# Openings of a two-layer encoder: who makes the first rests, which buffer holds the block that is fetched twice, when sums are requested, and the order of the second block product

## The chip, the cores and the metric

The kernel runs on one core of a Trainium2 chip. The metric is the time of one execution on the device, in microseconds (us). Three runs of the kernel before took 2184.75, 2187.49 and 2182.68 us, so the median is 2184.75 us. A further execution was recorded by the hardware profiler; all rows of traces below come from it.

## The reference, cut to what matters

A batch of one sequence with 512 frames of 1024 features gets 16 meta tokens in front (528 tokens) and goes through two layers, all in float32. Each layer is

```python
h = h + 0.5 * swiglu(rmsnorm(h, ffn1_norm[l]), ffn1_w_gate[l], ffn1_w_up[l], ffn1_w_down[l])
h = h + hybrid_mixer(rmsnorm(h, mix_norm[l]), w_in[l], ...)
h = h + 0.5 * swiglu(rmsnorm(h, ffn2_norm[l]), ffn2_w_gate[l], ffn2_w_up[l], ffn2_w_down[l])
```

where `swiglu(x, g, u, d)` is `(silu(x @ g) * (x @ u)) @ d` with an inner width of 2816, and the mixer multiplies its normed input by one wide matrix (queries, keys, values, two halves of a gated linear unit, two gates), runs stick-breaking attention and a gated convolution beside each other, and merges them. A last RMS norm follows, and the meta tokens are dropped.

## The kernel before, in words

**Precision.** The activations lie transposed, 8 tiles of 128 features by 528 tokens. Every float32 operand is split into a rounded part (`hi`) and the rest (`lo`), and a product is three matrix products: hi by hi, hi by lo, lo by hi. For activations the parts are called `uh`/`ul` (of the input), `sh`/`sl` (of sums of input pieces) and `ah`/`al` (of the inner layer); for weights `wh`/`wl`, in rings of four tiles each, 128 x 1024. A raw weight tile `wr` (a ring of three, 512 KB each) comes from HBM by a DMA that SyncE (SP) issues. ScalarE (ACT) rounds it (line 80, CAST wh<-wr). The rest comes in one of two ways. In `split` VectorE (DVE) subtracts (line 81, wl<-wr,wh). In the other way ACT writes the negated rounded part into `wl` (line 255) and GpSimd (POOL) issues a DMA that fetches the same weights from HBM a second time and adds them there (line 257, wl<-wg, wl<-wu or wl<-win). Mixer weights take the second way throughout.

**Seven products for eight.** The first two matrices of an FFN, and the value and gate halves of the mixer's linear unit, are computed in a scheme with seven block products. Input and weights are cut in two along the 1024 features and in column pairs, which gives weight blocks w11, w12, w21, w22 (each entry holds the block of both matrices, 8 x 128 columns). The seven weight operands are w11, s1 = w11 + w12, s2 = s1 + w22, w21, s3 = w12 + w22, w22, s4 = s2 + w21. A sum of two blocks is made by DMA: SP loads one block into a tile, POOL adds the other from HBM to it (line 207). The third block is added by DVE in place (line 267, s<-s,wr or wr<-wr). One block product is 24 matrix products of 264 columns (256 in the last FFN).

**The openings.** A new input is normed before each FFN or mixer, and what needs the norm factor can't be evicted at once. So at five places the first two column groups, numbered 0 and 1 here, are interleaved (`pair`, from line 422). Their w11 and w21 are called o11 and o21. The list `OPENING` (line 116) gives the order of the 14 block products; TensorE (PE) follows it as written:

o11 of 0, o11 of 1, o21 of 0, s1 of 0, s2 of 0, o21 of 1, w22 of 0, s3 of 0, s1 of 1, s4 of 0, s2 of 1, s3 of 1, w22 of 1, s4 of 1.

In the text they are o11_0, o11_1 and so on. The five openings are called A (mixer of layer 0), B (second FFN of layer 0), C (first FFN of layer 1), D (mixer of layer 1), E (second FFN of layer 1). The first FFN of layer 0 starts in another way.

After s2_n, DVE forms a combination from the PSUM accumulator in two halves (`opposite`, line 461: pe<-pb,q, or be<-bb,q in the mixer). The product w22_n accumulates on top of it, so PE can't start w22_n before both halves stand. The accumulator that `opposite` read is then written on by s3_n, so s3_n must wait for the two halves as well. `begin` (line 454) and `kept` (line 449) are ACT copies between accumulators.

**What sets the order.** Each engine runs its instructions in the order of its own list. PE's list is as written in the openings and in the mixer's attention. The other lists, and PE's in `down` (the FFN's second matrix), come from a scheduler that goes by priorities and its own estimates; `tc.add_manual_dep(..., NOSYNC)` puts one instruction behind another without a wait. Weights are prepared ahead by a walk over the list of products: `prep_unit` handles the product three places ahead (`LOOK`), and `fetch` keeps three raw tiles on their way or in use (`RAW`). In an opening the raw ring holds, in this order, o11_0, o11_1, o21_0, w11 for s1_0 (with w12 added by POOL), w22_0, o21_1, then w21 for s4_0 a second time, w22_1 and w21 for s4_1 a second time. s1_0 stays in its raw tile until s4_0. Sums s3_0, s1_1 and s3_1 go to tiles `s` of their own, requested by `fetch_sums` (line 230): s3_0 before the opening, s1_1 and s3_1 together, then the next quad's s1 and s3 together. In before.py the rests of o11_0, o11_1 and o21_0 are made by POOL's adding DMAs, that of o21_1 by DVE.

Of the kernel before, what the change touches and what calls it, by code (L numbers as in the profile page):

```python
# [13 lines left out]
P = 128  # L14
# [47 lines left out]
def kernel(ctx, tc, hT, par, const, wg1, wu1, wd1, win, wao, wco, wout, wg2, wu2, wd2, out):  # L62
# [35 lines left out]
    def fn(out, in_, func, **kw):  # L98
        need = SETS[func]
        if table["set"] != need:  # L100
            load = act.preload_act_table_set(need)
            for p in table["acts"]:
# [14 lines left out]
               ("s4", 0), ("s2", 1), ("s3", 1), ("w22", 1), ("s4", 1))  # L117
# [56 lines left out]
    state = {"prep": 0, "use": 0, "fetch": 0, "out": 0, "sums": 0}  # L174
# [14 lines left out]
    for n, (key, src, nk) in enumerate(units):  # L189
        at = key[1:]  # L190
        if nk == "w11":
            later_sums.append((n, ("s1", "s3")))
# [37 lines left out]
    def fetch_sums():  # L230

        n, names = later_sums[min(state["sums"], len(later_sums) - 1)]
        _, *at = units[n][0]
        if state["sums"] == len(later_sums) or tuple(at[:2]) != quads["of"]:
            return
        state["sums"] += 1
        for name in names:
            bufs = 1 if name == "s1" and at[0] == 2 else 2
            t = quads["pool"].tile([P, 8, P], F32, tag=name, bufs=bufs, name=name)
            load(t, n, "w11" if name == "s1" else "w22", "w12")  # L240
            raws[(name, *at)] = t

    def prep_unit():
# [7 lines left out]
        if nk not in QUAD:  # L251
            raw, nk0, nk = raws[key], nk, 8 if nk in OPEN else nk
            if key[0] in MIXER or nk0 == "o11" or nk0 == "o21" and units[n - 1][2] == "o11":
# [7 lines left out]
        else:  # L261
            at = key[1:]
            if nk == ("s1" if at in opened else "w11"):
                fetch_sums()
            if nk in ("s2", "s4"):
                x, y = raws[("s1", *at)], raws[("w22" if nk == "s2" else "w21", *at)]
                dve.tensor_tensor(out=x, in0=x, in1=y, op=ALU.add)  # L267
# [7 lines left out]
    def unit(*key):  # L275
        while state["prep"] < min(len(units), state["use"] + 1 + LOOK):
# [145 lines left out]
    def pair(ptile, sp, st, mode, of, ats, between, take, done):  # L422
# [23 lines left out]
        def kept(c):  # L446
            t = sp.tile([P, 2, TH], F32, tag="q", bufs=2, name="q")
            with priority(-URGENT):
                copies.append(act.copy(t, v(c)))
            return t  # L450

        def begin(c, t):
            with priority(-URGENT):
                copies.append(act.copy(v(c), t))

        copies = []
# [858 lines left out]
```

## Time and profile before

| | us |
|---|---|
| runs of the kernel before | 2184.75 (2182.68 to 2187.49) |
| the profiled execution, whole | 2186.04 |
| its span, first to last instruction | 2184.2 |
| PE busy | 2135.3 (98 %) |
| DVE busy | 1586.8 (73 %) |
| ACT busy | 1183.1 (54 %) |
| POOL busy | 534.4 (24 %) |

| opening | first to last product, us | length |
|---|---|---|
| A, mixer of layer 0 | 369.35 to 424.54 | 55.19 |
| B, second FFN of layer 0 | 740.38 to 788.09 | 47.71 |
| C, first FFN of layer 1 | 1100.92 to 1155.24 | 54.32 |
| D, mixer of layer 1 | 1467.54 to 1520.04 | 52.50 |
| E, second FFN of layer 1 | 1820.69 to 1871.15 | 50.46 |

The ends are the starts of the first product of the opening and of the first one behind it. In rows of waits the columns are total us, times, longest us. In rows of time the columns are start, duration, engine, line, operation, output<-input, shape; what stands in square brackets is the idle time of the engine just before it and what ended it. SPq is SP's queue of DMA issues.

### The profile page before, as it was taken

How to read it: one execution, taken by the hardware profiler on the slowest of the kernel's cores; microseconds unless marked ns; L12 is line 12 of the kernel's file. 1: busy time of each engine (PE TensorE's matmuls, PEld its weight loads, DVE VectorE, ACT ScalarE, POOL GpSimd, SP SyncE). 2: the span in 40 equal slices, each digit the busy share in tenths (PEclk: the TensorE clock that was granted, in tenths of full speed). 3: DMA queues.
4: the chain of work that ended last, by engine and by line, in shares of the span. 5: the costliest groups of instructions: out<-in, count | busy, mean ns of one | idle time of the engine just before them, and what ended most of it. 6: DMA issues, size and time to landing. Idle time of an engine off the chain costs nothing.

```text
span 2184.2 us, 40061 instructions
## 1 busy us (share of the span) xinstructions
PE 2135.3 (98%) x16058; PEld 2047.1 (94%) x16058; DVE 1586.8 (73%) x2221; ACT 1183.1 (54%) x1672; POOL 534.4 (24%) x499
## 2 busy tenths in 40 slices
PE   9999999999999999999989999999999999999998
PEld 9999999899999999999989999998888888899897
DVE  6867687777776677667877666877787767776685
ACT  6434356567776645343553443465678775343354
POOL 1322321311111231323123223213112112322220
PEclk9999999999999999999999999999999999999999
DMA  7465447765578957464395655367656789575532
GB/s 223 137 167 139 133 109 212 179 143 119 131 168 183 214 156 186 128 164 123 94 218 154 166 137 153 100 183 197 154 122 135 188 184 227 154 177 140 158 103 82
DMA packets 155290, 340.64 MB, mean 156 GB/s; under 512 B 17248, under 2 KB 21472, under 8 KB 155104
## 3 DMA queue, kind: packets, MB, share of 16 engines
q1 hardware_dynamic: 110928, 235.27, 34.2%
q0 software_dynamic: 43488, 102.26, 27.4%
q8 instruction: 126, 2.06, 0.4%
q10 hardware_dynamic: 688, 0.55, 0.1%
q14 instruction: 60, 0.49, 0.1%
HBM read 331.59 MB, written 6.42 MB: 155 GB/s over the span
## 4 chain that ended last, share of the span: by engine, by line
PE 89%; DMA 5%; DVE 3%; ACT 1%; issue 1%; SPq 0%; DVEq 0%; ACTq 0%; POOL 0%; POOLq 0%
PE pb L725 14%; PE ps L725 14%; PE ps L861 13%; PE ps L292 11%; PE ps L847 10%; PE pb L292 5%; PE pe L292 5%; PE pe L725 5%; DMA wr<-wu 2%; PE ps L443 1%; DMA wr<-win 1%; PE z L1043 1%; PE bs L443 1%; PE po L1087 1%; PE pe L443 1%
## 5 line engine op out<-in xcount | busy, mean ns | idle before, releaser
L80 ACT CAST wh<-wr 128x1024 fp32r<-128x1024 f32 (+4 forms) x284 | 251.6, 892 | 374.2 <-PE ps L292 90.7
L81 DVE TENSOR_TENSOR wl<-wr,wh 128x1024 fp32r<-128x1024 f32 (+4 forms) x284 | 312.6, 1103 | 62.4 <-ACT wh L80 59.1
L80 ACT CAST wh<-s 128x1024 fp32r<-128x1024 f32 x171 | 179.4, 1049 | 299.0 <-DVE s L267 85.8
L81 DVE TENSOR_TENSOR wl<-s,wh 128x1024 fp32r<-128x1024 f32 x171 | 233.0, 1362 | 52.5 <-ACT wh L80 50.1
L781 POOL TENSOR_TENSOR h<-h,dt 128x528 f32<-128x528 f32 (+1 forms) x96 | 177.7, 1858 | 268.4 <-DVE dt L779 268.4
L861 PE MATMUL ps<-uh,wh 128*128 128x264 f32 (+1 forms) x664 | 207.9, 313 | 0.3 <-DVE q L961 0.3
L861 PE MATMUL ps<-uh,wl 128*128 128x264 f32 (+1 forms) x664 | 203.6, 307 | 0.1
L861 PE MATMUL ps<-ul,wh 128*128 128x264 f32 (+1 forms) x664 | 203.7, 307 | 0.0
L207 POOL DMA_DIRECT2D s<-wg x81 | 73.1, 903 | 532.7 <-DMA s<-wg 202.0
L889 DVE SCALAR_TENSOR_TENSOR y<-uc,prm,y 128x528 f32<-128x528 f32 (+1 forms) x240 | 185.9, 811 | 0.5
L725 PE MATMUL ps<-ul,wh 128*128 128x264 f32 (+1 forms) x576 | 163.7, 284 | 0.0
L725 PE MATMUL pb<-sl,wh 128*128 128x264 f32 (+1 forms) x576 | 163.3, 283 | 0.0
L725 PE MATMUL ps<-uh,wl 128*128 128x264 f32 (+1 forms) x576 | 163.3, 283 | 0.0
L725 PE MATMUL pb<-sh,wl 128*128 128x264 f32 (+1 forms) x576 | 163.2, 283 | 0.0
L725 PE MATMUL pb<-sh,wh 128*128 128x264 f32 (+1 forms) x576 | 162.9, 283 | 0.0
L725 PE MATMUL ps<-uh,wh 128*128 128x264 f32 (+1 forms) x576 | 162.6, 282 | 0.0
L254 ACT CAST wh<-wr 128x1024 fp32r<-128x1024 f32 x103 | 108.0, 1049 | 95.1 <-PE ps L861 40.5
L292 PE MATMUL ps<-ah,wh 128*128 128x264 f32 (+1 forms) x616 | 142.7, 301 | 3.2 <-ACT wh L80 2.7
L292 PE MATMUL ps<-al,wh 128*128 128x264 f32 (+1 forms) x616 | 141.9, 300 | 0.5 <-DVE al L81 0.5
L292 PE MATMUL ps<-ah,wl 128*128 128x264 f32 (+1 forms) x616 | 141.7, 300 | 0.0
L861 PEld LDWEIGHTS ps<-uh,wl 128*128 128x128 f32 x664 | 125.0, 188 | 6.1 <-DMA wl<-win 0.3
L861 PEld LDWEIGHTS ps<-uh,wh 128*128 128x128 f32 x664 | 124.9, 188 | 6.2 <-issue 0.5
(402 smaller groups left out, 6918.1 us busy)
## 6 DMA issues: line engine op xcount, KB each, us to landing
wr<-wd SPq DMA_DIRECT2D x96, 384.0 KB, 3.6
wr<-wg SPq DMA_DIRECT2D x135, 256.0 KB, 3.5
wr<-wu SPq DMA_DIRECT2D x135, 256.0 KB, 3.8
wr<-win SPq DMA_DIRECT2D x56, 512.0 KB, 3.9
wl<-win POOLq DMA_DIRECT2D x56, 512.0 KB, 7.7
s<-wg SPq DMA_DIRECT2D x81, 256.0 KB, 4.8
s<-wu SPq DMA_DIRECT2D x81, 256.0 KB, 5.7
s<-wg POOLq DMA_DIRECT2D x81, 256.0 KB, 5.3
```

What stands on the lines that cost most here:

```text
L80: i = act.copy(hi, x)
L81: dve.tensor_tensor(out=lo, in0=x, in1=f(hi), op=ALU.subtract)
L207: queue.dma_start(raw[:, a:b], src, **kw)
L254: act.copy(hi[:, :nk], raw[:, :nk])
L292: pe.matmul(ps[:, c, :n], wt[:, k0 + k, :], xt[:, s:s + n], start=(k == 0 and pi == 0), stop=(k == end and pi == 2))
L443: pe.matmul(ps[:, e, :TH], wt[:, 4 * e + kk, :], xt, start=start and kk == 0 and pi == 0, stop=kk == KH - 1 and pi == 2, skip_group_check= ...
L725: pe.matmul(ps[:, e, :TH], wt[:, 4 * e + kk, :], xt, start=start and kk == 0 and pi == 0, stop=kk == 3 and pi == 2, skip_group_check=True)
L781: pool.tensor_tensor(out=tri(h[j], mode), in0=tri(h[j], mode), in1=tri(t, mode), op=ALU.add)
L847: pe.matmul(ps, wt[:, k0 + k, :], xt[:, s], start=(n == 0 and pi == 0), stop=(n == nk - 1 and pi == 2))
L861: pe.matmul(ps, wt[:, k, :], xt[:, s], start=(n == 0 and pi == 0), stop=(n == KD - 1 and pi == 2))
L889: t = dve.scalar_tensor_tensor(out=y, in0=uc[i][:, c0 + k:k + T], scalar=col(w0 + k), in1=y, op0=ALU.mult, op1=ALU.add)
L1043: pe.matmul(z[:, hh, :n], kk[r, ks], qq[r, q0:q0 + n], start=(pi == 0), stop=False, skip_group_check=True)
```

## The change

It has five parts, all on the openings, and one beside them.

1. The rests of o11_0 and o11_1 are made by `split`, so by DVE; ACT's negated copy and POOL's adding DMA for these two fall away. While these two units are asked for, the walk looks two places ahead and not three.
2. w21 for s4_0 is requested by `fetch_sums` into a tile `s` right behind s3_0, ahead of the opening, and no longer takes a raw tile. Tag s1 has two tiles everywhere, tag s3 one in the mixer. w21 for s4_1 is fetched at the place of s1_1 in the walk.
3. `fetch_sums` takes a count: s1_1 is requested when s2_0 is prepared, s3_1 with s3_0, and at s2_1 and s4_0 one and two sums of the quads that follow.
4. `OPENING` has s2_1 ahead of s4_0.
5. Three orders without waits: DVE's addition for s4 stands behind `opposite`; ACT's rounding of s2_0, s2_1 and s4_1 stands behind the last `begin`; that of s3_0 behind the norm's exponential (of s3_1 no longer).
6. `down` is issued on PE as written (but for each FFN's last group). On PE's list this moves four matrix products of `down` out of each of the openings B, C and E, where they stood ahead of s3_1, to the place behind the opening.

```diff
     OPENING = (("o11", 0), ("o11", 1), ("o21", 0), ("s1", 0), ("s2", 0), ("o21", 1), ("w22", 0), ("s3", 0), ("s1", 1),
-               ("s4", 0), ("s2", 1), ("s3", 1), ("w22", 1), ("s4", 1))
+               ("s2", 1), ("s4", 0), ("s3", 1), ("w22", 1), ("s4", 1))
+    WHEN = {("s2", "s1"): 1, ("s3", "w22"): 1, ("s4", "s2"): 2}
...
-        elif nk == "s1" and at in opened:
-            first = units[n - 1][2] in OPEN
-            later_sums.append((n, ("s3",) if first else ("s1", "s3")))
-            fetches += [(n, key, nk)] if first else []
-        elif at in opened and nk in ("s2", "s4"):
-            fetches.append((n, ("w22" if nk == "s2" else "w21", *at), "w22" if nk == "s2" else "w21"))
+        elif at in opened and nk in QUAD:
+            if nk == "s1" and units[n - 1][2] in OPEN:
+                later_sums += [(n, "s3"), (n, "w21")]
+                fetches.append((n, key, nk))
+            elif nk == "s1":
+                later_sums += [(n, "s1"), (n, "s3")]
+                fetches.append((n, ("w21", *at), "w21"))
+            elif nk == "s2":
+                fetches.append((n, ("w22", *at), "w22"))
...
+    def fetch_sums(count):
+
+        for n, name in later_sums[state["sums"]:state["sums"] + count]:
+            _, *at = units[n][0]
+            if tuple(at[:2]) != quads["of"]:
+                return
+            state["sums"] += 1
+            tag = "s3" if name == "s3" else "s1"
+            bufs = 1 if name == "s3" and at[0] == 2 else 2
+            t = quads["pool"].tile([P, 8, P], F32, tag=tag, bufs=bufs, name=tag)
+            load(t, n, *{"s1": ("w11", "w12"), "s3": ("w22", "w12")}.get(name, (name,)))
+            raws[(name, *at)] = t
...
-            if key[0] in MIXER or nk0 == "o11" or nk0 == "o21" and units[n - 1][2] == "o11":
+            if key[0] in MIXER or nk0 == "o21" and units[n - 1][2] == "o11":
                 act.copy(hi[:, :nk], raw[:, :nk])
                 act.activation(lo[:, :nk], raw[:, :nk], AF.Copy, scale=-1.0)
...
-            if nk == ("s1" if at in opened else "w11"):
-                fetch_sums()
+            if at in opened:
+                fetch_sums(WHEN.get((nk, units[n - 1][2]), 0))
+            elif nk == "w11":
+                fetch_sums(2)
             if nk in ("s2", "s4"):
                 x, y = raws[("s1", *at)], raws[("w22" if nk == "s2" else "w21", *at)]
-                dve.tensor_tensor(out=x, in0=x, in1=y, op=ALU.add)
+                i = dve.tensor_tensor(out=x, in0=x, in1=y, op=ALU.add)
+                if nk == "s4" and at in opened:
+                    tc.add_manual_dep(i.ins, state["opposite"].ins.name, NOSYNC, reason="behind the combination")
             i = split(raws[("s1" if nk in ("s2", "s4") else nk, *at)], hi, lo)
-            if nk == "s3" and at in opened:
-                tc.add_manual_dep(i.ins, state["rsqrt"].ins.name, NOSYNC, reason="behind the norm")
+            if at in opened and units[n - 1][2] in ("s1", "w22"):
+                behind = state["rsqrt" if nk == "s3" else "begin"]
+                tc.add_manual_dep(i.ins, behind.ins.name, NOSYNC, reason="behind the norm")
...
+        state["look"] = LOOK - 1
         ws = [unit("o11", *of, at) for at in ats]
+        state["look"] = LOOK
...
-                        down(gi)
+                        with tc.manual_schedule(engines={mybir.EngineType.PE}):
+                            down(gi)
```

**DVE in opening C, around the combination of group 0.** In the kernel before (s_13327 is s3_0, s_13338 is s1_1, the raw tile in `wr<-wr` is s1_0, to which w21 is added for s4_0):

```order
L81 TENSOR_TENSOR wl<-s_13327,wh 128x1024
L648 TENSOR_TENSOR up<-ps,g 128x264
L461 SCALAR_TENSOR_TENSOR pe<-pb,q 128x264
L267 TENSOR_TENSOR wr<-wr 128x1024
L461 SCALAR_TENSOR_TENSOR pe<-pb,q 128x264
L81 TENSOR_TENSOR wl<-s_13338,wh 128x1024
```

In the changed kernel (s_13333 is s3_0, s_13439 is s1_1, s_13338 now holds w21 for s4_0):

```order
L81 TENSOR_TENSOR wl<-s_13333,wh 128x1024
L469 SCALAR_TENSOR_TENSOR pe<-pb,q 128x264
L658 TENSOR_TENSOR up<-ps,g 128x264
L469 SCALAR_TENSOR_TENSOR pe<-pb,q 128x264
L81 TENSOR_TENSOR wl<-s_13439,wh 128x1024
L273 TENSOR_TENSOR wr<-wr,s_13338 128x1024
```

The addition for s4_0 moved from between the two halves of the combination to behind them. B and E read alike. In A and D, the mixer's openings, the rest of s1_1 stands between the two halves now:

```order
L81 TENSOR_TENSOR wl<-s_4579,wh 128x1024
L469 SCALAR_TENSOR_TENSOR be<-bb,q 128x264
L81 TENSOR_TENSOR wl<-s_4685,wh 128x1024
L469 SCALAR_TENSOR_TENSOR be<-bb,q 128x264
L273 TENSOR_TENSOR wr<-wr,s_4584 128x1024
```

Here s_4579 is s3_0, s_4685 is s1_1 and s_4584 is w21 for s4_0; the addition left that place in A and D too.

**POOL ahead of opening C.** In the kernel before (wl_13136 and wl_13209 are the rests of o11_0 and o11_1, wr_13141 is s1_0, wl_13263 the rest of o21_0, s3_13327 and s1_13338 the sums s3_0 and s1_1):

```order
L257 DMA wl_13136<-wg1 128x512
L257 DMA wl_13136<-wu1 128x512
L207 DMA wr_13141<-wg1 128x512
L207 DMA wr_13141<-wu1 128x512
L257 DMA wl_13209<-wg1 128x512
L257 DMA wl_13209<-wu1 128x512
L257 DMA wl_13263<-wg1 128x512
L257 DMA wl_13263<-wu1 128x512
L207 DMA s3_13327<-wg1 128x512
L207 DMA s3_13327<-wu1 128x512
L207 DMA s1_13338<-wg1 128x512
```

In the changed kernel (wr_13149 is s1_0, wl_13269 the rest of o21_0, s3_13333 and s1_13439 are s3_0 and s1_1):

```order
L211 DMA wr_13149<-wg1 128x512
L211 DMA wr_13149<-wu1 128x512
L261 DMA wl_13269<-wg1 128x512
L261 DMA wl_13269<-wu1 128x512
L211 DMA s3_13333<-wg1 128x512
L211 DMA s3_13333<-wu1 128x512
L211 DMA s1_13439<-wg1 128x512
```

Four adding DMAs of 256 KB each are gone from POOL's list ahead of each opening.

**SP in opening C.** In the kernel before (s3_13327 is s3_0, s1_13338 is s1_1, s3_13343 is s3_1, s1_13547 the next quad's s1, wr_13447 is w21 for s4_0, the fetch that stands first in the raw ring behind the sums):

```order
L207 DMA s3_13327<-wg1 128x512
L207 DMA s3_13327<-wu1 128x512
L207 DMA s1_13338<-wg1 128x512
L207 DMA s1_13338<-wu1 128x512
L207 DMA s3_13343<-wg1 128x512
L207 DMA s3_13343<-wu1 128x512
L207 DMA s1_13547<-wg1 128x512
L207 DMA s1_13547<-wu1 128x512
L207 DMA wr_13447<-wg1 128x512
L207 DMA wr_13447<-wu1 128x512
```

In the changed kernel (s1_13338 is w21 for s4_0, s1_13439 is s1_1, s3_13520 is s3_1, wr_13451 is w21 for s4_1):

```order
L211 DMA s3_13333<-wg1 128x512
L211 DMA s3_13333<-wu1 128x512
L211 DMA s1_13338<-wg1 128x512
L211 DMA s1_13338<-wu1 128x512
L211 DMA s1_13439<-wg1 128x512
L211 DMA s1_13439<-wu1 128x512
L211 DMA s3_13520<-wg1 128x512
L211 DMA s3_13520<-wu1 128x512
L211 DMA wr_13451<-wg1 128x512
L211 DMA wr_13451<-wu1 128x512
```

w21 for s4_0 moved up by three sums, s1_1 and s3_1 down by one place; the next quad's s1 stands behind these rows now.

More of the change, by code (lines that the diff above doesn't have):

```diff
@@ L173 @@
     RAW = 3
-    state = {"prep": 0, "use": 0, "fetch": 0, "out": 0, "sums": 0}
+    state = {"prep": 0, "use": 0, "fetch": 0, "out": 0, "sums": 0, "look": LOOK}
     ready, raws, counted = {}, {}, set()
@@ L275, in unit @@
     def unit(*key):
-        while state["prep"] < min(len(units), state["use"] + 1 + LOOK):
+        while state["prep"] < min(len(units), state["use"] + 1 + state["look"]):
             if units[state["prep"]][2] in QUAD and quads["pool"] is None:
@@ L460, in opposite @@
                 with priority(-URGENT):
[L461 to L462 removed]
+                    state["opposite"] = dve.scalar_tensor_tensor(out=out[:, e, :TH], in0=c[:, e, :TH], scalar=-1.0,
+                                                                 in1=q[:, e], op0=ALU.mult, op1=ALU.add)
         As = [ptile() for _ in range(2)]
+        state["look"] = LOOK - 1
         ws = [unit("o11", *of, at) for at in ats]
+        state["look"] = LOOK
         for ks in (range(KH - 1), (KH - 1,)):
@@ L470, in pair @@
         begin(Bs[0], v(As[0]))
-        between(ptile("pe"), copies[0])
+        between(ptile("pe"), state["begin"])
         Bs.append(kept(As[1]))
```

25 lines of the change are left out of this document (6 added, 19 removed).

## The prediction, made before any run of the changed kernel

> **What bounds the kernel now.** PE is busy for 98% of the span, so only its idle or slowed time can be won. I first read PE's waits over the whole span (total us, times, longest):
>
> ```profile
> PE pe L443 <- DVE pe L461: 12.2, 3, 4.9
> PE be L443 <- DVE be L461: 7.4, 2, 4.0
> PE bs L443 <- DMA wl<-win: 5.2, 4, 2.2
> PE ps L292 <- ACT wh L80: 2.7, 3, 0.9
> PE bs L443 <- DVE be L461: 2.0, 2, 1.0
> PE ps L443 <- DMA wl<-wg: 2.0, 1, 2.0
> ```
>
> Nearly all of it is line 443, the openings. Next I read one window per opening, A to E (start:end, length, busy time and instructions of PE, PEld, DVE, ACT, POOL, granted clock, DMA share, GB/s):
>
> ```profile
> 369.35:424.54 55.19, 47.50 (x343) 46.72 (x342) 39.35 (x63) 28.42 (x39) 15.30 (x19) 0.88 0.74 191
> 740.38:788.09 47.71, 43.10 (x344) 42.26 (x345) 36.53 (x56) 25.28 (x39) 12.18 (x14) 1.00 0.94 227
> 1100.92:1155.24 54.32, 47.16 (x346) 46.29 (x345) 38.15 (x59) 26.29 (x39) 12.36 (x14) 0.91 0.90 217
> 1467.54:1520.04 52.50, 45.29 (x343) 44.30 (x341) 38.97 (x59) 28.62 (x39) 15.38 (x18) 0.93 0.74 193
> 1820.69:1871.15 50.46, 44.30 (x341) 43.28 (x340) 37.00 (x57) 25.92 (x39) 12.25 (x14) 0.93 0.90 222
> ```
>
> The lengths add to 260.2 us, and B, which never lost the clock, is the shortest. The two largest rows of waits, 12.2 + 7.4 = 19.6 us, are one place in each opening, PE's first product of w22_0 (idle time ahead of it in brackets):
>
> ```profile
> 397.45 0.56 PE L443 MATMUL be<-sh,wh 128*128 128x264 f32 x1 [3.96 <-DVE be L461]
> 762.49 0.36 PE L443 MATMUL pe<-sh,wh 128*128 128x264 f32 x1 [3.30 <-DVE pe L461]
> 1127.44 0.56 PE L443 MATMUL pe<-sh,wh 128*128 128x264 f32 x1 [3.99 <-DVE pe L461]
> 1492.65 0.56 PE L443 MATMUL be<-sh,wh 128*128 128x264 f32 x1 [3.42 <-DVE be L461]
> 1843.89 0.55 PE L443 MATMUL pe<-sh,wh 128*128 128x256 f32 x1 [4.90 <-DVE pe L461]
> ```
>
> What DVE waited for there shows in C, from DVE's timeline:
>
> ```profile
> 1119.63 1.23 DVE L81 TENSOR_TENSOR wl<-s,wh 128x1024 fp32r<-128x1024 f32 x1 [0.58 <-ACT wh L80]
> ...
> 1121.12 0.43 DVE L461 SCALAR_TENSOR_TENSOR pe<-pb,q 128x264 f32<-128x264 f32 x1
> 1125.72 1.23 DVE L267 TENSOR_TENSOR wr<-wr 128x1024 f32<-128x1024 f32 x1 [4.17 <-DMA wr<-wu]
> 1126.86 0.43 DVE L461 SCALAR_TENSOR_TENSOR pe<-pb,q 128x264 f32<-128x264 f32 x1
> ```
>
> The first half of the combination stands at 1121.55, the second at 1127.29. Between them DVE's list holds the addition for s4_0, which no one needs yet; it waits 4.17 us for w21, fetched a second time. SP asked for that block late, once a raw tile was free:
>
> ```profile
> 1116.36 0.33 SPq L207 DMA_DIRECT2D wr<-wg  x1
> ```
>
> The wait costs more than its idle time. In the chain of waits the block product behind it takes 5.62 us where the next takes 3.02 us, a loss of 2.6 us; the first products of w22_0 in A, C, D and E are of the long kind (0.55 to 0.56 us), B's is not (0.36 us). The last row is s4_0:
>
> ```profile
> 1127.44 5.62 PE pe L443 x24
> 1133.06 3.02 PE pb L443 x24
> ...
> 1139.01 2.80 PE pb L443 x23
> ```
>
> **The change, part by part.** *1. w22_0 starts earlier* (own tile for w21 of s4_0, its addition behind both halves, fewer adding DMAs, o11 by DVE). Once that addition has left, what is late next is the rest of s3_0, which DVE makes ahead of the first half, and in A and D that of s1_1, now between the halves. Both follow an ACT rounding of a sum; these are the binding ones, s1_1 in A and D, s3_0 in B, C, E:
>
> ```profile
> 393.19 1.05 ACT L80 CAST wh<-s 128x1024 fp32r<-128x1024 f32 x1 [2.72 <-DMA s<-win]
> 755.23 1.05 ACT L80 CAST wh<-s 128x1024 fp32r<-128x1024 f32 x1 [1.92 <-DMA s<-wu]
> 1118.55 1.05 ACT L80 CAST wh<-s 128x1024 fp32r<-128x1024 f32 x1 [0.97 <-DMA s<-wu]
> 1490.19 1.04 ACT L80 CAST wh<-s 128x1024 fp32r<-128x1024 f32 x1 [2.85 <-DMA s<-win]
> 1838.96 1.04 ACT L80 CAST wh<-s 128x1024 fp32r<-128x1024 f32 x1 [5.62 <-PE ps L443]
> ```
>
> Four of them waited for the DMA that brings the sum. Lower bound, sums landing as before: in A the rounding ends at 394.24, the rest takes 1.23, the last half 0.43, so PE could start at 395.9 in place of 397.45, a gain of 1.5. D likewise: 1490.19 + 1.04 + 1.23 + 0.43 = 1492.9, so -0.2. In B, C and E three DVE pieces of 0.43 follow the rest (the row left out in C's fence is the third): C can start at 1118.55 + 1.05 + 1.23 + 1.29 = 1122.1, a gain of 5.3, E at 1842.5, a gain of 1.4. In B this gives 758.8, ahead of the end of o21_1 on PE (762.49 - 3.30 = 759.2), so the gain is its wait, taken as 3.5 with what moves ahead of it. Together 11.5.
>
> Upper bound: no wait is left, 19.6, and no slow product behind it, 4 x 2.6 = 10.4, so 30; with the stalls at o11, 5.2 + 2.0 = 7.2, it is 37.
>
> Between them decides what the DMA queues gain. In the 55 us of 1080 to 1135 they held (queue, packets, MB, share of the time of 16 engines):
>
> ```profile
> q0 software_dynamic: 2466, 4.49, 47.3%
> q1 hardware_dynamic: 3979, 7.24, 40.3%
> ```
>
> POOL's adding transfers (q0) cost 55 x 0.473 / 4.49 = 5.8 us per MB, SP's loads (q1) 55 x 0.403 / 7.24 = 3.1. The change drops two adding transfers of 0.52 MB ahead of each opening, 6.1 us, and puts w21 (0.52 MB, 1.6 us) ahead of s1_1: net 4.5 us. That counts where the queues are full, in A, C and D:
>
> ```profile
> 375.00:380.00 5.00, 4.49 (x22) 4.28 (x22) 3.59 (x7) 2.42 (x5) 0.00 (x0) 0.54 1.08 315
> 740.00:745.00 5.00, 4.62 (x38) 4.65 (x39) 4.82 (x7) 3.02 (x6) 0.00 (x0) 1.00 0.79 180
> 1093.00:1101.00 8.00, 8.00 (x68) 8.00 (x67) 6.25 (x12) 7.03 (x11) 5.28 (x6) 1.00 1.01 199
> ```
>
> At the starts of A and C the share is over 1.0, in B 0.79; the sums of B and E I leave where they land. I give A and D 3.0 us, two thirds of the relief, since part of it is spent ahead of transfers that are not late; so A gains 4.5 and D 2.8. In C the sums then come before o21_1 has ended (1127.44 - 3.99 = 1123.45); that end moves by the stall at o11_1 and its slow products:
>
> ```profile
> 1105.51 0.36 PE L443 MATMUL ps<-uh,wl 128*128 128x264 f32 x1 [2.00 <-DMA wl<-wg]
> 1106.05 0.42 PE L443 MATMUL ps<-uh,wl 128*128 128x264 f32 x1
> ```
>
> That is 2.0 of wait and about 0.8 of products, to 1120.6: C gains 6.8. Sum of the five: 4.5 + 3.5 + 6.8 + 2.8 + 1.4 = 19.0. The stalls at o11 lie ahead of w22_0 in the same opening, so they aren't counted again. To this comes the clock: 2.6 us in each of A, C and D, whose waits get short, 7.8 at most; I take 5, because a short wait can slow products too: behind the 2.00 us of C's o11 they took 0.42 us. E keeps 3.5 us of its wait and its slow product.
>
> The two added subtractions on DVE, 2 x 1.23 us, run ahead of each opening, where DVE is busy 6.25 of 8 us while PE is covered with other work, so I cost them at nothing; uncovered they cost up to 2.5 an opening (a rival below).
>
> The Trainium skill ("TensorE: Matmul & The Clock Gate", Part 1: The HAM clock gate) says that PE falls to half clock after an idle window of some 3.4 us. The rows agree in part: B's 3.30 us cost no clock, but 2.00 us did in C. By the page alone every wait that stays under 3.4 us would cost no clock, and the clock's gain would be 7.8 in place of 5, 10.4 if E's falls under it too, an estimate.
>
> *2. s2_1 ahead of s4_0.* s3_1 no longer follows directly on the halves of s2_1's combination; that hides the 2.0 us that A and D wait there. In B, C and E the 2.7 us of line 292 are matrix products of `down` that stood in the opening and waited for a weight; they leave it, for the place behind the opening, where I expect no such wait since the weight comes in its old order on ACT. Together 4.7. Against it: in A and D the query weights behind the opening take this chain, whose transfer's median landing stands in the page's list of issues (KB, us):
>
> ```profile
> 415.47 1.05 ACT L255 ACTIVATE wl<-wr 128x1024 fp32r<-128x1024 f32 x1
> 416.82 0.88 POOL L257 DMA_DIRECT2D wl<-win  x1 [2.42 <-ACT wl L255]
> ```
>
> ```profile
> wl<-win POOLq DMA_DIRECT2D x56, 512.0 KB, 7.7
> ```
>
> 416.82 + 7.7 (the median landing) = 424.5, just as A ends at 424.54: it is already due at its last moment, so the 1.0 us that s3_1 gains in each is waited for here instead. So 4.7 - 2.0 = 2.7.
>
> *3. `down` as written.* The products moved out run behind the opening instead: their PE time moves, 0.
>
> *4. s2_1 one place sooner.* Its weight is s1_1 plus w22_1, so it waits for w22_1's landing. In C DVE makes that sum here:
>
> ```profile
> 1129.20 1.22 DVE L267 TENSOR_TENSOR s<-s,wr 128x1024 f32<-128x1024 f32 x1 [0.43 <-DMA wr<-wu]
> ```
>
> s2_1 takes the place of s4_0, which PE began at 1139.0; with C's gain of 6.8 and its 2.6 of clock it is due at 1129.6. Sum, rounding and rest take 1.22 + 1.05 + 1.23 = 3.5. With the landing as now the weight stands at 1132.7, 3.1 late, the upper bound. But w22_1 now has the raw tile that w21 had, requested at 1116.36 and landed by 1125.72: ready at 1129.2, with 0.4 to spare, the lower bound 0. The second is nearer, since the raw ring does lose a fetch; I take -0.7.
>
> **Sum:** 19.0 + 5 + 2.7 - 0.7 = 26. The profiled execution took 2186.04 us (span 2184.2 and 1.8 around it), 1.3 over the median; so 2186.0 - 26 = 2160.0 there, and 2158.7, given as 2159, against the median.
>
> **Rivals.** *The wait changes hands.* The sums land no earlier than before, because SP and POOL hold other transfers ahead of them. Then w22_0 waits for s3_0 or s1_1, 11.5 is gained, the slow products stay, and with parts 2 and 4 (2.7 - 0.7) it is 13.5: 2184.75 - 13.5 = 2171. For it: four of the five roundings waited for their sum's DMA. Against it: the shares over 1.0.
>
> *All hidden.* The upper bound, 37, and 4.7 - 0.7, gives 41: 2144. For it: POOL loses four adding DMAs of 256 KB ahead of the sums. Against it: E's binding rounding ends at 1840.0, after which 1.23 + 1.29 must still run on DVE, so a wait of some 3.5 us there goes only if its sum lands sooner, for which no full queue speaks.
>
> *Slower: later sums.* In DVE's list the two added subtractions (2.5 us) stand ahead of the norm's sums (`nsum`, line 377), behind which SP asks for s3_0 and what follows. If they push that back in full, and w21 goes ahead of s1_1 (1.6), the sums come up to 4.1 us later in all five openings: 11.5 + 2.7 - 0.7 - 5 x 4.1 = -7, so 2192. It decides from 13.5 / 5 = 2.7 us on. Against it: DVE's 1.75 idle us of 8 ahead of C take most of the 2.5, and 6.1 us of dropped transfers outweigh 1.6.
>
> *It doesn't do what it says.* The transfer of w21 into its own tile waits for that tile's last reader and lands as late as before; then the addition moves but s4_0 waits for it, one place behind: the gain is 0 to 4.
>
> **Chances.** Forecast (2152 to 2168) 0.48; wait changes hands 0.20; all hidden 0.18; later sums 0.07; no effect 0.07. A measurement of this kernel tells about 0.2%, 4.4 us, from no change; so faster 0.48 + 0.20 + 0.18 = 0.86, the same 0.07, slower 0.07. The range takes in both neighbours, 2142 to 2174.
>
> **What would show it.** In the changed kernel the row of PE waiting for line 469 (461 before) should fall from 19.6 to below 7 us, DVE should make the two halves of the combination within 1 us of each other in B, C and E, and the opening windows should add to some 235 us with a clock near 1.00 in A, C and D. It is wrong if PE then waits as long for `wl` of s3_0 or s1_1 (first rival), if s3_1 or w22_1 show new waits above 1 us, if new waits come up behind the openings, or if `nsum` falls later against PE's o11_0 than before (the slower rival).

## The result, and the profile after

Four runs of the changed kernel took 2163.81 to 2170.57 us, median 2167.68, beside 2184.47 us for the kernel before: a ratio of 0.9921, with a 95% interval of 0.9901 to 0.994. The gain is 17 us where 26 were forecast, and the time lies at the upper edge of the forecast's 2152 to 2168. The profiled execution took 2168.47 us (span 2166.7), 17.6 less than that of before.

The five opening windows of the changed kernel, from the first product of each to the first one behind it (columns as in the prediction):

```profile
371.85:420.12 48.27, 43.99 (x343) 43.18 (x342) 39.77 (x64) 28.10 (x39) 14.18 (x19) 0.96 0.75 195
738.50:782.83 44.33, 42.00 (x341) 41.60 (x341) 36.34 (x56) 24.86 (x39) 10.52 (x12) 1.00 0.90 220
1098.05:1143.71 45.66, 43.17 (x343) 42.99 (x341) 37.83 (x59) 26.00 (x39) 11.37 (x13) 0.96 0.94 230
1458.32:1503.81 45.49, 42.59 (x343) 41.68 (x342) 39.52 (x59) 28.10 (x39) 12.25 (x18) 1.00 0.77 200
1806.38:1851.74 45.36, 40.78 (x339) 40.28 (x338) 36.39 (x57) 25.63 (x39) 11.36 (x13) 1.00 0.95 223
sum 229.11, PE 212.52 PEld 209.73 DVE 189.85 ACT 132.69 POOL 59.68; mean PE 42.50 PEld 41.95 DVE 37.97 ACT 26.54 POOL 11.94
```

They add up to 229.1 us where they were 260.2: 31.1 us gained. That is more than the 25 of the forecast's sign (some 235 us) and than the 28 that its terms inside the openings add to. The span is only 17.5 us shorter, so everything outside the openings is 13.6 us longer. PE's waits over the span of the changed kernel say what those are:

```profile
PE pe L452 <- DVE pe L469: 7.0, 3, 3.2
PE ps L301 <- DVE up L658: 5.0, 3, 1.9
PE ps L711 <- ACT wh L80: 4.9, 1, 4.9
PE ps L872 <- DMA wl<-win: 3.7, 2, 1.9
PE bs L452 <- ACT bs L463: 2.4, 2, 1.6
PE ps L452 <- ACT ps L463: 2.4, 2, 1.4
PE be L543 <- ACT nt L80: 1.9, 1, 1.9
PE ps L301 <- ACT ah L80: 1.6, 1, 1.6
PE be L452 <- DVE be L469: 1.4, 2, 1.2
PE be L543 <- DVE nt L81: 1.2, 2, 0.6
```

The first and the ninth row are w22_0's wait: 7.0 + 1.4 = 8.4 in place of 19.6. Two rows had no match before and lie behind the openings: `down` (line 301) waits 5.0 us for `up`, and the first query product (line 872) 3.7 us for the rest of its weights. Inside the openings s2_1 waits 2.4 + 2.4 for ACT's `begin` copy (line 463), and the norm's sum waits 3.1 for `nt` (line 543). The 4.9 us of line 711, the kernel's start, stood at 5.0 before.

The first product of w22_0 in the five openings of the changed kernel:

```profile
394.78 0.36 PE L452 MATMUL be<-sh,wh 128*128 128x264 f32 x1 [0.20 <-DVE be L469]
758.08 0.36 PE L452 MATMUL pe<-sh,wh 128*128 128x264 f32 x1 [1.34 <-DVE pe L469]
1118.68 0.36 PE L452 MATMUL pe<-sh,wh 128*128 128x264 f32 x1 [2.49 <-DVE pe L469]
1479.21 0.36 PE L452 MATMUL be<-sh,wh 128*128 128x264 f32 x1 [1.17 <-DVE be L469]
1827.27 0.36 PE L452 MATMUL pe<-sh,wh 128*128 128x256 f32 x1 [3.15 <-DVE pe L469]
```

Measured from the start of its opening, w22_0 begins earlier by:

| opening | before | after | gain | forecast |
|---|---|---|---|---|
| A | 28.10 | 22.93 | 5.2 | 4.5 |
| B | 22.11 | 19.58 | 2.5 | 3.5 |
| C | 26.52 | 20.63 | 5.9 | 6.8 |
| D | 25.11 | 20.89 | 4.2 | 2.8 |
| E | 23.20 | 20.89 | 2.3 | 1.4 |
| sum | | | 20.1 | 19.0 |

Outside the openings the kernel lost 2.5 us ahead of A, 2.5 behind A, 2.4 behind B, 2.3 behind C, 1.9 behind D and 1.9 behind E (lengths from the end of one opening to the start of the next). Of the losses behind B, C and E, 1.8 us in all are the products of `down` that left the openings (four of 264 columns in B and in C, two of 512 in E).

**Behind A** the changed kernel's rows of ACT, POOL and PE read:

```profile
410.83 1.05 ACT L80 CAST wh<-s 128x1024 fp32r<-128x1024 f32 x1 [3.71 <-DVE s L273]
411.78 1.05 ACT L258 CAST wh<-wr 128x1024 fp32r<-128x1024 f32 x1
...
414.40 0.87 POOL L261 DMA_DIRECT2D wl<-win  x1
...
422.44 0.39 PE L872 MATMUL ps<-uh,wl 128*128 128x264 f32 x1 [1.93 <-DMA wl<-win]
```

The adding DMA for the first query weights was issued at 414.40, 5.7 us ahead of the end of the opening (7.7 in the kernel before), and PE could go on 8.0 us after the issue. The rounding of s4_1 (410.83) stands ahead of this chain on ACT.

**Behind B**, the rows of DVE, ACT, SP and PE:

```profile
773.11 1.22 DVE L273 TENSOR_TENSOR s<-s,wr 128x1024 f32<-128x1024 f32 x1
774.44 1.05 ACT L80 CAST wh<-s 128x1024 fp32r<-128x1024 f32 x1 [2.91 <-DVE s L273]
...
777.78 0.38 SPq L211 DMA_DIRECT2D wr<-wd  x1
...
784.63 0.62 ACT L80 CAST wh<-wr 128x512 fp32r<-128x512 f32 x1 [2.18 <-DMA wr<-wd]
785.16 0.42 ACT L105 ACTIVATE g<-g 128x264 f32<-128x264 f32 x1
785.89 0.43 DVE L658 TENSOR_TENSOR up<-ps,g 128x264 f32<-128x264 f32 x1
...
786.38 0.39 PE L301 MATMUL ps<-ah,wh 128*128 128x264 f32 x1 [1.93 <-DVE up L658]
```

Read from below: PE's next product of `down` waits until DVE's `up` (785.89 to 786.32) has read the last accumulator `ps` of the opening. `up` needs `g` from ACT's Silu, and that Silu (785.16) stands behind the rounding of `down`'s fourth weight tile, which waited 2.18 us for its DMA; SP had asked for that tile only at 777.78, 5.1 us ahead of the end of the opening (782.83). The tile's place in the raw ring came free late, since the rounding of the first `down` weights stands on ACT behind that of s4_1 (774.44), and that waited 2.91 us for DVE's addition. The addition (773.11) stands behind the combination after s2_1: the new order was written for every s4, not only for s4_0. The experiments test this reading.

### The profile page after: what moved, and what is told of

Same layout as the page of the kernel before. It is cut to its first block, busy times and chain, and to the rows that moved or that the text cites. A ratio compares the mean times of both kernels' runs of the same rounds, so it can differ in the third digit from the quotient of the medians.

```text
span 2166.7 us, 40018 instructions
## 1 busy us (share of the span) xinstructions
PE 2124.8 (98%) x16058; PEld 2038.0 (94%) x16058; DVE 1593.8 (74%) x2231; ACT 1172.0 (54%) x1662; POOL 513.6 (24%) x479
## 4 chain that ended last, share of the span: by engine, by line
PE 85%; DMA 6%; DVE 6%; ACT 1%; issue 1%; POOL 0%; SPq 0%; DVEq 0%; ACTq 0%; POOLq 0%
PE pb L735 14%; PE ps L735 14%; PE ps L872 13%; PE ps L301 10%; PE ps L858 10%; PE pe L735 5%; PE pe L301 4%; PE pb L301 4%; DVE wl L81 2%; DMA wr<-wd 1%; PE z L1054 1%; DMA s<-wu 1%; PE po L1098 1%; DMA wr<-wu 1%; DMA wr<-win 1%
## 5 line engine op out<-in xcount | busy, mean ns | idle before, releaser
L80 ACT CAST wh<-wr 128x1024 fp32r<-128x1024 f32 (+4 forms) x294 | 261.5, 898 | 356.0 <-PE ps L301 98.9
L81 DVE TENSOR_TENSOR wl<-wr,wh 128x1024 fp32r<-128x1024 f32 (+4 forms) x294 | 322.2, 1099 | 61.3 <-ACT wh L80 58.5
L80 ACT CAST wh<-s 128x1024 fp32r<-128x1024 f32 x171 | 179.3, 1049 | 296.9 <-DVE s L273 101.4
L301 PE MATMUL ps<-ah,wh 128*128 128x264 f32 (+1 forms) x616 | 143.0, 302 | 6.5 <-DVE up L658 5.0
L258 ACT CAST wh<-wr 128x1024 fp32r<-128x1024 f32 x93 | 97.6, 1049 | 92.2 <-PE ps L872 38.8
L301 PE MATMUL ps<-al,wh 128*128 128x264 f32 (+1 forms) x616 | 142.4, 301 | 0.4 <-DVE al L81 0.4
L301 PE MATMUL ps<-ah,wl 128*128 128x264 f32 (+1 forms) x616 | 142.3, 301 | 0.0
```

Source lines behind the costliest of these rows:

```text
L80: i = act.copy(hi, x)
L81: dve.tensor_tensor(out=lo, in0=x, in1=f(hi), op=ALU.subtract)
L258: act.copy(hi[:, :nk], raw[:, :nk])
L301: pe.matmul(ps[:, c, :n], wt[:, k0 + k, :], xt[:, s:s + n], start=(k == 0 and pi == 0), stop=(k == end and pi == 2))
```

## The experiments

Each time is a median beside the kernel before on the same chip (2184.5 to 2185.7 us). Ratios are to the kernel before, with the 95% interval. The rows come from several chips, and where the intervals of two rows overlap, their difference in us is not clear of the noise.

| kernel | us | ratio | interval |
|---|---|---|---|
| changed kernel | 2167.68 | 0.9921 | 0.9901 to 0.9940 |
| changed kernel, again | 2165.51 | 0.9908 | 0.9894 to 0.9922 |
| before, addition behind the combination | 2170.58 | 0.9937 | 0.9913 to 0.9961 |
| the same for s4_0 alone, and o11 by DVE | 2171.18 | 0.9938 | 0.9922 to 0.9955 |
| changed, o11 by DMA | 2172.66 | 0.9941 | 0.9919 to 0.9964 |
| changed, old order of products | 2173.88 | 0.9945 | 0.9930 to 0.9960 |
| changed, first query weights by DVE | 2162.80 | 0.9904 | 0.9883 to 0.9926 |
| changed, only s4_0 behind the combination | 2163.05 | 0.9899 | 0.9872 to 0.9925 |
| both repairs | 2158.97 | 0.9878 | 0.9863 to 0.9892 |
| both repairs, again | 2159.58 | 0.9873 | 0.9855 to 0.9890 |
| both repairs, old order of products | 2173.34 | 0.9946 | 0.9928 to 0.9963 |
| both repairs, o21_0 by DVE | 2158.07 | 0.9871 | 0.9858 to 0.9885 |

### One order alone

```diff
-                dve.tensor_tensor(out=x, in0=x, in1=y, op=ALU.add)
+                i = dve.tensor_tensor(out=x, in0=x, in1=y, op=ALU.add)
+                if nk == "s4" and at in opened:
+                    tc.add_manual_dep(i.ins, state["opposite"].ins.name, NOSYNC, reason="behind the combination")
...
-                    dve.scalar_tensor_tensor(out=out[:, e, :TH], in0=c[:, e, :TH], scalar=-1.0, in1=q[:, e],
-                                             op0=ALU.mult, op1=ALU.add)
+                    state["opposite"] = dve.scalar_tensor_tensor(out=out[:, e, :TH], in0=c[:, e, :TH], scalar=-1.0,
+                                                                 in1=q[:, e], op0=ALU.mult, op1=ALU.add)
```

> The kernel before with one order added: DVE's addition for s4 stands behind both halves of the combination, nothing else of the change. My theory (the addition's place on DVE's list caused the wait at w22_0; the late second fetch of w21 alone does little harm): w22_0 starts as early as the sums allow, so the lower bound of the forecast's first term comes, 11.5 us, and some of the clock; PE's wait for the two halves falls from 19.6 to about 8, the total by 10 to 14 us. Rival (the late fetch itself is what costs; it needs a tile of its own): DVE then waits for w21 one place later, s4_0 stalls in its place, total within 4 us of before.

2170.58 us, 15 less than before: nearly the whole gain of the change from one order. The profiled execution of this kernel was the fastest of its four (2166.57 us). PE's waits in this kernel (the combination is line 463 here, `down` line 294):

```profile
PE ps L294 <- ACT wh L80: 6.0, 3, 2.1
...
PE bs L445 <- DMA wl<-win: 4.8, 4, 2.2
PE bb L445 <- DVE c L463: 4.5, 2, 2.7
PE pb L445 <- DVE c L463: 3.9, 3, 1.6
PE pe L445 <- DVE pe L463: 3.3, 3, 2.2
```

The wait at w22_0 fell from 19.6 to 3.3, further than the 8 expected. Part of it turned up one place later, as 4.5 + 3.9 = 8.4 us at s4_0, which waits for the combination after s3_0 (`c`): ahead of it DVE's list holds the two additions for s4_0 and s2_1, whose blocks come from the raw ring, and several rests. The wait of the products of `down`, which here still stand in B, C and E, grew from 2.7 to 6.0 us; in the next kernel, where only s4_0 is held back, it is 2.4.

### The order and the split, with w21 still fetched late

Edits to the kernel before (with `state["opposite"]` set as above):

```diff
-            if key[0] in MIXER or nk0 == "o11" or nk0 == "o21" and units[n - 1][2] == "o11":
+            if key[0] in MIXER or nk0 == "o21" and units[n - 1][2] == "o11":
...
+                if nk == "s4" and at in opened and units[n - 1][2] != "w22":
+                    tc.add_manual_dep(i.ins, state["opposite"].ins.name, NOSYNC, reason="behind the combination")
```

> The kernel before with two edits: only s4_0's addition stands behind the combination, and the rests of o11_0 and o11_1 are made by DVE; w21 is still fetched late, in the raw ring. My theory (of the change's parts the addition's place and the split do nearly all; the own tile's gain is what DVE then waits for w21 ahead of s3_0's combination, 8.4 us in the kernel with the one order alone): the waits at o11, 6.3 us there, go, the 8.4 stay; 4 to 7 us below that kernel's 2170.6, about 2165. Rival (with PE earlier still, the late w21 costs all that the split brings): 2169 to 2173.

2171.18 us, in the rival's range. In the profile PE has no wait for a DMA at o11 any more, and the wait for `c` grew from 8.4 to 11.1 us:

```profile
PE pb L445 <- DVE c L463: 9.5, 3, 3.4
...
PE bb L445 <- DVE c L463: 1.6, 1, 1.6
```

So 2.7 of the 6.3 us saved at o11 are waited for at s4_0, and another 2.7 at the norm's sum (`nt`, line 535). The clock took its share too: the mean granted clock of this execution was 0.994, that of the one order's profile 0.998, and behind the longest wait for `c` (3.41 us, in B) 18 products took 4.00 us at a clock of 0.50. How much of the loss the late w21 makes alone is not separated. With w21 in a tile of its own the row is 0.5 to 3.2 us in the two kernels with the old order of products (below), and with s4_0 one place later, as in the changed kernel, it is gone. So w22_0 itself gets its gain without the own tile; it is s4_0 that waits without it. The own tile alone was not tried.

### o11 by DMA again

```diff
-            if key[0] in MIXER or nk0 == "o21" and units[n - 1][2] == "o11":
+            if key[0] in MIXER or nk0 == "o11" or nk0 == "o21" and units[n - 1][2] == "o11":
```

> The changed kernel, but the rests of o11_0 and o11_1 come by ACT's negated copy and POOL's adding DMA again. My theory (the split removes the 7.2 us of waits at o11 and their slow products, and relieves the DMA queues ahead of the sums): the waits at o11 come back with 5 to 7 us and w22_0 waits some 3 to 5 us longer in A, C and D together; total 8 to 15 us above the changed kernel, 2175 to 2182. Rival (the start of w22_0 is set by the sums alone, stalls at o11 ahead of it are absorbed there): total within 4 us of the changed kernel's 2167.7.

2172.66 us, 5.0 above the changed kernel's 2167.68: below my 8 to 15, a little above the rival's 4, and with intervals that overlap, so the size of this difference is not settled. The waits at o11 came back (4.5 for `win`, 0.9 for `wu`), and w22_0 waits 5.4 + 5.4 = 10.8 in place of 8.4. But the split has a price of its own that the forecast set at nothing: in the changed kernel the norm's sum (line 543) waits 3.1 us for `nt` on ACT and DVE in A and D; with o11 by DMA that wait is gone, and only a first product of s1_0 waits 1.0 us for `nt`.

### The old order of block products

```diff
-               ("s2", 1), ("s4", 0), ("s3", 1), ("w22", 1), ("s4", 1))
-    WHEN = {("s2", "s1"): 1, ("s3", "w22"): 1, ("s4", "s2"): 2}
+               ("s4", 0), ("s2", 1), ("s3", 1), ("w22", 1), ("s4", 1))
+    WHEN = {("s2", "s1"): 1, ("s3", "w22"): 1, ("s4", "s1"): 1, ("s2", "s4"): 2}
```

> The changed kernel with the old order of block products: s4_0 ahead of s2_1 (the sums of the following quads are then asked for at s4_0 and s2_1, one and two). My theory (the swap costs: ACT's copy that begins s2_1's accumulator stands behind roundings on ACT's list, PE waits 4.8 us for it in A, B, D and E): these waits go, in exchange the 2.0 us at s3_1 in A and D come back, and four products of `down` stand in each of B, C and E again; total 0 to 4 us below the changed kernel, 2164 to 2168. Rival (the swap brings the 4.7 us that I forecast): 3 to 5 us above it, 2171 to 2173.

2173.88 us, 6.2 above the changed kernel; the interval overlaps that of the changed kernel's first measurement, and not that of its second. My theory fell: s2_1's waits for `begin` went as expected, but more came back elsewhere. The same edit on top of the two repairs below:

> Both repairs, and the old order of block products. If the swap costs as much as it brings, it comes out within 3 us of the kernel with both repairs alone; by my theory 0 to 3 us below it, 2155 to 2158, by the rival of the swap (it brings 4.7) 3 to 5 us above it, 2161 to 2163.

2173.34 us, 14.4 above the kernel with the repairs alone. The waits of that last kernel:

```profile
PE bs L452 <- DVE be L469: 5.2, 2, 2.8
...
PE ps L301 <- ACT wh L80: 3.4, 3, 1.6
PE pb L452 <- DVE c L469: 3.2, 2, 2.1
```

s3_1's wait in A and D is 5.2 us and not the 2.0 of the kernel before, the products of `down` wait inside the openings again, and s4_0 waits for `c`. The forecast of +4.7 for the swap was too low. The edit isn't a pure swap, since the places at which sums are asked for, and one order on ACT, hang on the same list.

This kernel also corrects the account of the change. With the old order the products of `down` stand ahead of s3_1 again, although `down` is issued as written. And with part 6 of the change left out, the lists of ACT, DVE, POOL and SP are the same as in the changed kernel, and PE's differs only in the order of some products of `down` among themselves, right behind B, C and E; that kernel was not run. So it is the swap that moved these products out of the openings.

### The two losses behind the openings

First the rest of the first query weights by DVE:

```diff
-            if key[0] in MIXER or nk0 == "o21" and units[n - 1][2] == "o11":
+            if key[0] in MIXER and key[:1] + key[2:] != ("q", 0) or nk0 == "o21" and units[n - 1][2] == "o11":
```

> The changed kernel, but the rest of the first query weights of each mixer is made by DVE's subtraction, not by POOL's adding DMA. My theory (behind openings A and D PE waits for this DMA, 1.93 + 1.76 us, and its products run slow behind it, 4.56 and 5.41 in place of 2.92): both go, 6 to 8 us less than the changed kernel, about 2161. Rival (the raw weights or their rounding come as late, or the next weights take over the wait): less than 2 us gained.

2162.80 us, 4.9 below the changed kernel; its profile has no wait of line 872 for a DMA, only

```profile
PE ps L872 <- DVE q L972: 0.7, 1, 0.7
```

The gaps behind A and D in this profile are 315.8 and 300.8 us, as in the kernel before (315.8 and 300.7); in the changed kernel they were 318.4 and 302.6.

Then the order for s4_0 alone:

```diff
-                if nk == "s4" and at in opened:
+                if nk == "s4" and units[n - 1][2] == "s2":
```

> The changed kernel, but only the addition for s4_0 stands behind the combination, not that for s4_1. My theory (s4_1's addition waits for the end of s2_1, ACT's rounding of it waits for the addition, and the weights of what follows the opening stand behind it on ACT's list; so the weights of `down` are prepared late, its fourth weight tile is requested late, and ACT's Silu stands behind its rounding): PE's waits for `up` behind B, C and E, 5.0 us in the changed kernel, fall below 1, and 5 to 7 us are gained, about 2162. Rival (the DMAs or the raw ring of three set the weights' pace there, the order does not matter): within 2 us of the changed kernel and the waits for `up` stay.

2163.05 us, 4.6 below. The waits for `up` nearly vanished, 5.0 to 0.8, and in B the rounding of the fourth `down` tile waits for PE, not for its DMA, with the Silu behind it 0.7 us after the end of the opening (780.44), where it was 2.3 in the changed kernel and 0.7 in the kernel before:

```profile
PE ps L301 <- DVE up L658: 0.8, 3, 0.3
...
780.56 0.62 ACT L80 CAST wh<-wr 128x512 fp32r<-128x512 f32 x1 [0.59 <-PE ps L452]
781.11 0.43 ACT L105 ACTIVATE g<-g 128x264 f32<-128x264 f32 x1
```

The gaps behind B, C and E are 0.7, 0.7 and 1.0 us longer than in the kernel before, of which 0.6 each are the moved products; in the changed kernel it was 2.4, 2.3 and 1.9. The gaps behind A and D are shorter too, 316.5 and 300.9 us, though the query weights' DMA is issued only 0.3 us sooner against the end of the opening (6.1 us ahead of it); the rest there is landing and clock of one execution, so what the two edits gain can't be told apart exactly. No DMA was added or dropped in this kernel, so it was the order on DVE, not the queues, that made `down` late. The interval of each of these two overlaps that of the changed kernel; that of both together does not:

> The changed kernel with both repairs: the first query weights' rest by DVE, and only s4_0's addition behind the combination. My theory (two separate places behind the openings, A and D, and B, C and E): the gains of the two add up, 4.9 + 4.6 us, total about 2158, and PE's waits for the query weights and for `up` are both below 1 us. Rival (PE ahead of time only waits longer for the sums in the next opening): 2162, with more wait at w22_0.

2158.97 us, a ratio of 0.9878 (0.9863 to 0.9892). The waits behind the openings are 0.8 us and none for the query weights; what is left stands inside the openings:

```profile
PE pe L452 <- DVE pe L469: 8.0, 3, 3.4
...
PE bs L452 <- ACT bs L463: 2.8, 2, 1.5
PE be L452 <- DVE be L469: 2.5, 2, 1.3
...
PE ps L301 <- DVE up L658: 0.8, 3, 0.3
```

Both kernels were then run once more side by side, in five rounds.

> The changed kernel itself, beside the others of this call on the same chip: 2167 to 2169, 0.992 of the kernel before; its waits behind the openings (3.7 for the query weights, 5.0 for `up`) are there again, and the 1.57 us near 60 us, if that wait comes from the change and not from this execution.

> The kernel with both repairs, beside the changed one on the same chip: 8 to 10 us below it, about 2159; if its lead came from the chip and not from the two repairs, within 4 us of it.

2165.51 and 2159.58 us. The lead is 5.9 us here, less than the 8 to 10 expected and the 8.7 of the first time; the intervals of the ratios, 0.9894 to 0.9922 and 0.9855 to 0.9890, don't meet. In the changed kernel's second profile the waits behind the openings are there again (5.1 for `up`, 3.7 for the query weights). A single profile has its own spread, though: here the openings add to 226.7 us, and the gap behind A is 320.5 and not 318.4.

Ahead of opening A there is a wait near 60 us, the row `PE ps L301 <- ACT ah L80`; it is 1.0 us here, 1.57 in the first profile of the changed kernel and 0.52 in the kernel before. It bears on the 2.5 us lost ahead of A in the first profile. From the end of that wait to A it is 310.6 us in the kernel before and in the second profile, 312.1 in the first: these 1.5 us are spread between executions of the same kernel. The other 1.0 us is the wait itself. It is at most 0.52 us in four profiles (the kernel before, the two experiments on it, and o11 by DMA) and 0.9 to 1.6 in the nine others, although no engine's list differs there. Whether the change makes it stays open.

### What holds up the last sum

```diff
-            if key[0] in MIXER and key[:1] + key[2:] != ("q", 0) or nk0 == "o21" and units[n - 1][2] == "o11":
+            if key[0] in MIXER and key[:1] + key[2:] != ("q", 0):
```

(on top of both repairs)

> The kernel with both repairs, and the rest of o21_0 made by DVE too: the last adding DMA of 0.52 MB ahead of the sums falls away in each opening. My theory (what is left of the wait at w22_0, 10.5 us with both repairs, is s3_0's landing, and that is set by the traffic on the DMA queues): s3_0 lands up to 3 us sooner in A, C and D, the wait falls to about 5, total 3 to 6 us below the kernel with both repairs, about 2154. Rival (one more subtraction on DVE ahead of the norm holds back more than the DMAs gain: the waits on `nt`, 3.0 there, and the sums' request): 0 to 4 us above it, 2159 to 2163.

2158.07 us, the same within the intervals. PE's waits:

```profile
PE pe L452 <- DVE pe L469: 7.7, 3, 2.9
...
PE be L543 <- DVE nt L81: 2.4, 2, 1.2
PE be L543 <- ACT nt L80: 1.7, 1, 1.7
...
PE be L452 <- DVE be L469: 1.2, 1, 1.2
```

w22_0 waits 8.9 us in place of 10.5 and 9.7 in the two profiles without this edit, and the waits on `nt` rose from 3.0 and 2.5 to 4.7. Neither theory got its number. What sets the landing of s3_0 stays open; the traffic of o21_0's adding DMA is at most a small part of it.

## Why the prediction was right, and where its size was off

The direction, the range and the cause were right: PE's stall at w22_0 came from the addition for s4_0 between the halves of the combination, and one order that moves it brings 15 us by itself. The forecast of 2159 missed 2167.7 by 9 us. Of its signs, the halves of the combination stand 0.7 us apart in B, C and E and the openings add to less than 235 us. But the wait at w22_0 fell to 8.4 and not below 7, the granted clock in A and C is 0.96, and one sign of being wrong came: new waits behind the openings. By its terms:

- **w22_0 earlier, 19.0.** Measured 20.1, opening by opening within 1.4 us. The bounds were right in kind: in C, PE went on waiting for the rest of s3_0, whose rounding started at 1115.20 when the sum had landed. That is the first rival, the wait that changes hands, at 8.4 of the 19.6 us. The bound of 11.5 holds for the changed kernel only, as the prediction has it: in A and D the rest of s1_1 stands between the halves there. I carried it over to the one order alone, which leaves no wait at w22_0 in A and D. And the stall at o11_1 in C had cost more than the 2.0 + 0.8 taken for it: the 28 products behind it took 5.06 us at a granted clock of 0.66, some 1.7 more than at full clock. C gained 5.9 all the same, since s3_0 held it.
- **Clock, 5.** The five products w22_0 took 24.4 us before and 16.5 after, by the starts of their neighbours: 8.0. E's came back too, which the forecast had left slow; C's kept 1.6 us of its loss.
- **s3_1 and `down`, 4.7, and s2_1, -0.7.** From the end of w22_0 to the end of the opening the five together got 3.0 us shorter, of which 1.8 are the products of `down` that only moved: 1.2 net where 4.0 were forecast. The term of -0.7 was mis-sized: s2_1 waits 4.8 us. It was priced on w22_1's landing; in A, B, D and E the wait is for ACT's `begin` copy (line 463).
- **Query weights, -2.0.** Right in kind: this chain was due at its last moment. PE lost 3.7 us of waiting and then products at a lower clock; the gaps behind A and D grew by 2.5 + 1.9 = 4.4. The DMA's issue came 2.0 us nearer to the end of the opening in both, not 1.0; 0.3 of that goes with the order for s4_1.
- **`down` behind the openings, 0.** This is the step that failed, in part 2's words "where I expect no such wait since the weight comes in its old order on ACT". The order on ACT was the old one, but the rounding of s4_1, which stands ahead of it, came late, since part 5 of the change puts the addition for every s4 behind the combination. The gaps behind B, C and E grew by 2.4 + 2.3 + 1.9 = 6.6, of which 1.8 is moved work: 4.8 lost. The prediction named what was queued behind the addition for s4_0, and never asked what is queued behind that for s4_1.

The openings thus gave 31.1 us, 29.3 without the moved products. Behind them 4.4 + 4.8 = 9.2 were given back where 2.0 were forecast, and 2.5 were lost ahead of A, which the forecast had no term for: 29.3 - 9.2 - 2.5 = 17.6, the difference of the two profiled times. Against the forecast that is 26 + 1.1 (w22_0) + 3.0 (clock) - 2.8 (s3_1, `down` and s2_1 in the openings) - 2.4 (query weights) - 4.8 (`down` behind them) - 2.5. Two terms came out better than forecast and hid part of the others, which is luck.

The list of changes ahead of the prediction gives the move of the products of `down` to part 6; it belongs to part 4, the swap, as the old order of products shows.

The slower rival, later sums, has a trace of truth: the split on DVE costs the 3.1 us at `nt`. It did not reach the sums' price of 2.7 us in each opening, and the last addition to `nsum` falls later against PE's first product in A alone (6.5 us behind it in place of 5.6).

## What to carry to other kernels

Before a stall is attacked by an order that holds one instruction back, list every instruction that the rule matches, and for each what stands behind it on its own engine and on the engine that reads it; here the rule meant for s4_0 also caught s4_1 and cost 5 us. When one engine is made faster in a stretch, price the first work behind the stretch as well: chains that were just in time there can come late. And undo parts on top of the best version too: going back to the old order of products, with what hangs on that list, cost some 6 us with the other losses in place, hardly clear of the noise, and 14 without them.

## What the runs showed of the hardware that was not expected

The length of PE's wait does not tell whether the products behind it run slow. In the changed kernel the windows of four groups of products right behind a wait (start:end, length, busy time and instructions by engine, granted clock, DMA share, GB/s):

```profile
1118.68:1123.22 4.54, 4.54 (x24) 4.54 (x25) 2.49 (x3) 1.04 (x1) 0.00 (x0) 0.62 1.09 276
1827.27:1830.18 2.91, 2.91 (x25) 2.91 (x25) 0.85 (x1) 1.05 (x1) 0.00 (x0) 1.00 1.10 248
422.44:427.00 4.56, 4.56 (x25) 4.56 (x25) 2.71 (x5) 1.40 (x2) 2.14 (x6) 0.63 1.04 265
786.38:789.39 3.01, 3.01 (x24) 3.01 (x25) 0.71 (x1) 0.61 (x1) 0.00 (x0) 1.00 0.89 181
```

A wait of 2.49 us was followed by a granted clock of 0.62, one of 3.15 us by full clock; a wait of 1.93 us was followed by 0.63 behind A and by full clock behind B. The Trainium skill ("TensorE: Matmul & The Clock Gate", Part 1: The HAM clock gate) says that the half clock comes after an idle window of about 3.4 us and that the window runs freely, so that the same kernel behaves differently from run to run. The spread agrees with a window that runs freely; that waits of 1.93 and 2.49 us cost clock does not fit a full idle window of 3.4 us, and here the measurement decides. For a forecast it means that the clock's share of a stall of 2 to 4 us is between nothing and some 2.5 us for the product behind it (1.6 in C of the changed kernel, 2.5 in C of the kernel before), and can't be told from the wait alone.

Much of the spread between executions of one kernel goes with this clock. The five executions of the kernel with both repairs, run again, took 2153.64 us at a mean granted clock of 0.998 at the one end and 2163.50 us at 0.994 at the other.
